# Norm squares added by VectorE, transposes one step later, and a rearranged end in a two-layer hybrid decoder

## The chip, the cores and the metric

The kernel runs on one core of a Trainium2 chip. The core's engines work side by side, each through its own queue in order: TensorE (PE, matmuls, with PEld for its weight loads), VectorE (DVE), ScalarE (ACT), GpSimd (POOL) and SyncE (SP, which here only issues DMAs). The metric is the device time of one execution in microseconds (us); the time of a kernel is the median of several executions. Traces show one profiled execution; its "span" runs from the first to the last instruction.

## The reference, cut to what matters

The input is a sequence of 512 tokens with 1024 channels in float32. Two layers run:

```
layer 0:  h = h + conformer_conv(rmsnorm(h))     # pw1 + GLU, causal depthwise conv of width 31,
                                                 # LayerNorm over channels, swish, pw2
          h = h + swiglu_ffn(rmsnorm(h))         # up 1024 -> 2*2816, silu(gate)*up, down
          k, v = rmsnorm(h) @ w_kv               # one shared K/V
layer 1:  q = rmsnorm(h) @ w_q                   # 16 heads of 64, 4 K/V heads
          s = q k^T / 8 + bias, window of 128 keys, in blocks of 128 queries over 256 keys
          p = exp(s - m) / (sum exp(s - m) + exp(sink - m))
          h = h + (p v) @ w_o
          h = h + swiglu_ffn(rmsnorm(h))
out = rmsnorm(h);   rmsnorm(x) = x * rsqrt(mean(x*x) + 1e-6) * gain
```

## The kernel before, in words

Channels lie on the 128 partitions, tokens along the free dimension: `h` is eight tiles of 128 x 512. Matmuls keep float32 accuracy by splitting both operands into a rounded high part and a low rest: `mm3` (lines 258-264) issues high*high (L262), high*low (L263) and low*high (L264). Weights arrive in chunks of 128 x 1024 (512 KB, DMA at L187); of each chunk ACT makes the high part `whi` (L203) and DVE the low part `wlo` (L204), three chunks ahead of their use. Activations are split by `split_scaled` (ACT L382, DVE L383) or `split` (ACT L386, DVE L387).

In layer 0 the tokens go in two halves of 256. While TensorE works on the first half's `pw2` and FFN, the depthwise convolution of the second half runs in the background: taps on DVE (L611), products on ACT (L603) that POOL adds up (L604), rows of the LayerNorm (L638, L640, L649). The background steps are traced between the weight chunks by due points.

A norm is gathered by the class `Rms`: for each of the eight tiles ACT squares it (L336) and `self.eng`, always POOL, adds it to the running sum (L340). `step1` turns the sum by two small matmuls on PE per half (L350) into a column, DVE scales it (L352), POOL raises it to -1/2 (L354), ACT makes a diagonal (L362); `step2` spreads it over the partitions by a matmul (L375) and ACT copies it out of PSUM (L369). `ffn_up` calls `step1` after the first pair of column blocks (four weight chunks).

Attention (`unit`, line 911) works on units of four heads and 128 queries, eight units for each half `gp` of the heads. A unit is a generator of four stages: scores (PE L927, DVE L930, into a score buffer `sc`, which POOL first gives the sinks, L920); exp with row sums (ACT L937), the reciprocal (DVE L939) and the scaling (POOL L941); transposes (PE L948) with their split (ACT L951, DVE L952); products with V (PE L262 to L264 with `vq`) and their split (ACT L966, DVE L967). `pipeline` (line 970) issues, in step t, the products of unit t-3, the transposes of unit t-2, the exp of unit t-1 and the scores of unit t. Eleven such steps per half; eight of them are traced between the matmuls of the q projection (or of the o projection's first part) and the last three follow behind, by `drain`. `sc` has two buffers. PSUM has eight banks, shared by all.

The end (`Fin`, line 1016) computes the last down projection for the two halves of tokens, `fa` and `fb`. `rows` adds each finished tile to `h` (DVE L1043), squares it (ACT L1047) and sums the squares: in `fa` all eight on POOL (L1049), in `fb` the first four on POOL, and the running sum and the last four go to PE, two small matmuls each (`total`, L1035). `sums` makes the factor (DVE L1066, POOL L1068, DVE diagonal L1070) and lets ACT scale `n_pool` tiles by the gain (L1075): 2 in `fa`, 3 in `fb`. `spread` (L1080) spreads the factor into a PSUM bank; ACT copies it to SBUF (L1082). `out_pool` multiplies the `n_pool` tiles on POOL by the copy (L1089), `out_dve` does the others on DVE straight from the bank (L1095); every tile is stored by a DMA (L1085) from SP, or from ACT for the `out_pool` tiles of `fb`. `fill` places steps of `fa.out_dve` behind given DVE instructions.

The order of the instructions on each engine is chosen by a planner that runs a timeline of its own and takes what is ready, earlier traced work first; semaphores are added by the framework. `issue_after(ins)` keeps what it encloses behind `ins` on the same engine. The framework also orders every two accesses of different engines to one PSUM bank as they were traced, reads among them.

Of the kernel before, what the change touches and what calls it, by code (L numbers as in the profile page):

```python
# [10 lines left out]
F32 = mybir.dt.float32  # L11
# [6 lines left out]
P = 128  # L18
# [3 lines left out]
KT = D // P  # L22
# [6 lines left out]
BAND = 2 * P  # L29
# [120 lines left out]
def hybrid_trunk(ctx: ExitStack, tc: tile.TileContext, xT, W, prm_in, wdw_in, sinks, relb, onehot, outT):  # L150
    nc = tc.nc
# [10 lines left out]
    def uid(s):  # L162
        ctr[0] += 1
        return f"{s}{ctr[0]}"

    def bank():
        return ps.tile([P, 512], F32, tag="bank", name=uid("bank"))
# [4 lines left out]
    def temp():  # L172
        return tmp.tile([P, 512], F32, tag="tmp", name=uid("tmp"))
# [92 lines left out]
    class Act:  # L266
        def __init__(self, n, w=512):
            self.per = 2048 // w
            self.q = [tuple(quads.tile([P, self.per, w], F32R, tag="quad", name=uid("quad")) for _ in range(2))
                      for _ in range(-(-n // self.per))]  # L270
# [6 lines left out]
    ALL = slice(0, S)  # L277
    HALF = (slice(0, 256), slice(256, 512))
# [31 lines left out]
    ones_m = cpool.tile([P, P], F32, tag="ones_m", name="ones_m")  # L310
# [14 lines left out]


    class Rms:
        def __init__(self, bc, tok=ALL):
            self.acc = None
            self.bc, self.tok, self.w = bc, tok, tok.stop - tok.start  # L330
            self.eng = nc.gpsimd
            self.stage = 0

        def add(self, t):
# [43 lines left out]
    def new_bc():  # L378
        return tmp.tile([P, 512], F32, tag="rsbc", name=uid("rsbc"), bufs=2)
# [123 lines left out]
        return hid  # L503

    class Next:
        def __init__(self, gains, x=None, bc=None, tok=ALL):
            self.gains, self.tok = gains, tok
            self.x, self.rms = x, None
            self.bc = bc

        def on_h(self, i):
            if self.x is None:
                self.x = {self.gains[0]: Act(KT)}
            if self.rms is None:
                self.bc = new_bc() if self.bc is None else self.bc
                self.rms = Rms(self.bc, self.tok)
            g = self.gains[0]
            split_scaled(cut(self.x[g][i], self.tok), h[i][:, self.tok], col(g, i))
            self.rms.add(h[i][:, self.tok])
# [28 lines left out]
    with tc.tile_pool(name="conv", bufs=2) as cv:  # L548
# [274 lines left out]
        job(second, (base, 0), (base + 8, 20), (base + 42, h1.n_steps - early))  # L823
        x0 = {"ffn0": Act(KT)}
        bc0 = new_bc()
        n0 = Next(("ffn0",), x0, bc0, HALF[0])
        pw2(h0.z, n0)
        ffn_part(0, 0, x0["ffn0"], HALF[0], n0.rms)
        flush()
# [2 lines left out]
    at = attn.enter_context(tc.tile_pool(name="attn", bufs=2))  # L832
# [25 lines left out]
    if True:  # L858
        ffn_part(0, 1, x0["ffn0"], ALL, Both(), nxt.on_h)
        x, rms = nxt.x, nxt.rms  # L860
# [18 lines left out]
        for half in range(2):  # L879
# [7 lines left out]
            if half == 0:  # L887
                rs_bc = rms.step2()
                rs = rms.rs
                for m in range(2):  # L890
                    t = temp()
# [4 lines left out]
        for n in range(4):  # L896
            t = temp()
# [13 lines left out]
        def unit(gp, jp, n):  # L911
            qt = slice(n * P, (n + 1) * P)
            k0 = max(n - 1, 0) * P
            nk = 1 if n == 0 else 2
            w = nk * P
            rows = [slice(HD * g, HD * (g + 1)) for g in range(2)]
            heads = [gp * 8 + g * 4 + 2 * jp + e for g in range(2) for e in range(2)]
            sc = at.tile([P, 4, 1 + BAND], F32, tag="sc", name=uid("sc"))
            sinks4 = sk.rearrange("p (a g j e) -> p a g j e", a=2, g=2, j=2)[:, gp, :, jp, :]
            nc.gpsimd.tensor_copy(sc[:, :, 0].rearrange("p (g e) -> p g e", g=2), sinks4)  # L920
            m4 = small.tile([P, 4], F32, tag="m4", name=uid("m4"))
            pbs = [bank().rearrange("p (a b) -> p a b", a=2) for _ in range(2)]
            for e in range(2):
                j = 2 * jp + e
                for a, b in ((0, 0), (0, 1), (1, 0)):
                    for g in range(2):
                        nc.tensor.matmul(pbs[g][:, e, :], qs[gp][a][rows[g], j, qt],  # L927
                                         kq[rows[g], b, gp, k0:k0 + BAND], start=a + b == 0, stop=a == 1)
            for u, hd in enumerate(heads):
                nc.vector.tensor_tensor_reduce(  # L930
                    sc[:, u, 1:1 + w], pbs[u // 2][:, u % 2, 0:w], bias[:, hd, BAND - w:BAND],
                    op0=ALU.add, op1=ALU.min, scale=1.0, scalar=sk[:, hd:hd + 1],
                    accum_out=m4[:, u:u + 1])
            yield
            sm = small.tile([P, 4], F32, tag="sm", name=uid("sm"))
            for j in range(4):
                nc.scalar.activation(sc[:, j, 0:1 + w], sc[:, j, 0:1 + w], AF.Exp, bias=m4[:, j:j + 1],  # L937
                                     scale=-1.0, accum_out=sm[:, j:j + 1])
            nc.vector.reciprocal(sm, sm)  # L939
            for j in range(4):  # L940
                nc.gpsimd.tensor_scalar(sc[:, j, 1:1 + w], sc[:, j, 1:1 + w], sm[:, j:j + 1], 0.0,  # L941
                                        op0=ALU.mult, op1=ALU.add)
            yield
            pts = []
            for kb_ in range(nk):
                pt = bank()
                for j in range(4):
                    nc.tensor.transpose(pt[:, j * P:(j + 1) * P], sc[:, j, 1 + kb_ * P:1 + (kb_ + 1) * P], ident)  # L948
                hi = at.tile([P, 512], F32R, tag="pth", name=uid("pth"), bufs=2)
                lo = at.tile([P, 512], F32R, tag="ptl", name=uid("ptl"), bufs=2)  # L950
                nc.scalar.copy(hi, pt)  # L951
                nc.vector.tensor_sub(lo, pt, f32(hi))  # L952
                pts.append((hi, lo))
            yield
            po = bank()[:, 0:BAND]
            for kb_ in range(nk):
                blk = k0 // P + kb_
                for g in range(2):
                    vs = [v[:, blk, gp, 2 * g:2 * g + 2, :].rearrange("p a c -> p (a c)") for v in vq]
                    mm3(po, vs, [pt[:, g * BAND:(g + 1) * BAND] for pt in pts[kb_]],  # L960
                        kb_ == 0 and g == 0, kb_ == nk - 1 and g == 1)
            if os_[gp] is None:
                os_[gp] = (quad(), quad())
            hi, lo = (o[:, 2 * jp:2 * jp + 2, qt] for o in os_[gp])
            src = po.rearrange("p (j q) -> p j q", j=2)
            nc.scalar.copy(hi, src)  # L966
            nc.vector.tensor_sub(lo, src, f32(hi))  # L967
            yield

        def pipeline(gp):  # L970
            units = [unit(gp, jp, n) for n in range(NBLK) for jp in range(2)]
            done = 0
            for t in range(len(units) + 3):
                for d in (3, 2, 1, 0):
                    if 0 <= t - d < len(units):
                        next(units[t - d])
                yield

        def drain(it):
# [36 lines left out]
    class Fin:  # L1016
        def __init__(self, hf):
            self.hf, self.tok = hf, HALF[hf]
            self.banks, self.hg = [bank() for _ in range(4)], []
            self.n_pool = 2 + hf  # L1020

        def down(self, kp, g):
            whi, wlo = get("down", 1, kp, g)
# [13 lines left out]

        def rows(self, g, other=lambda n, ins: None):

            n_add = 4 if self.hf else KT  # L1040
            for i in range(g * 4, g * 4 + 4):
                t = h[i][:, self.tok]
                add = nc.vector.tensor_add(t, self.banks[i // 2][:, (i % 2) * 256:(i % 2) * 256 + 256], t)  # L1043
                if i == KT - 1:
                    other(2, add.ins)
                sq = res.tile([P, 256], F32, tag="sq", name=uid("sq"), bufs=5)
                nc.scalar.square(sq, t)  # L1047
                if 0 < i < n_add:
                    nc.gpsimd.tensor_add(sq, self.acc, sq)  # L1049
                if i < n_add:  # L1050
                    self.run = self.acc = sq
                if not self.hf or i < n_add:
                    continue
                if i == n_add:
                    self.st = bank()
                self.total(sq, i == n_add, i == KT - 1)
                if i == KT - 2:
                    self.total(self.run, False, False)
# [19 lines left out]
        def spread(self):  # L1078
            self.pb = bank()[:, 0:256]
            nc.tensor.matmul(self.pb, ones_m, self.diag, start=True, stop=True)  # L1080
            self.bc = temp()[:, 0:256]
            nc.scalar.copy(self.bc, self.pb)  # L1082

        def store(self, i, t, q=nc.sync):
            q.dma_start(outT[i][:, self.tok], t)  # L1085
# [16 lines left out]
    fa = Fin(0)  # L1102
# [4 lines left out]
    fb = Fin(1)  # L1107
# [7 lines left out]
    for n, (kp, g) in enumerate(steps):  # L1115
        fb.down(kp, g)
        if n == 1:
            fa.sums()
        elif n == 2:
            fb.rows(0)  # L1120
            fa.spread()
        elif n == 3:
            fb.rows(1, fill)
    fa.out_pool()
    fb.sums(fill)
    fb.spread()
# [29 lines left out]
```

## Time and profile before

| | us |
|---|---|
| median of 3 executions | 1123.65 |
| lowest, highest | 1122.11, 1123.83 |
| the profiled execution | 1122.53 |
| its span | 1120.7 |
| PE busy in the span | 1103.7 (98%) |
| DVE, ACT, POOL busy | 663.5, 509.2, 324.0 |

The profiled execution lies 1.1 us under the median. In a group row of the profile, "x4 | 3.6, 952" means four instructions, 3.6 us busy in all, 952 ns each on average; what follows the next bar is the idle time of the engine ahead of them and what ended it. In a row of waits, "A <- B: 3.1, 1, 3.1" means A's engine sat idle until B was done: 3.1 us in all, once, 3.1 us at most. In a timeline row stand start, duration, engine, line, operation, output and inputs; a bracket gives the idle time before it. A row of a table of stretches gives the stretch, its length, then for PE, PEld, DVE, ACT and POOL the busy time and the number of instructions, then the TensorE clock granted, the DMA engines' share and GB/s. A queue's row (SPq, ACTq) counts DMA issues.

### The profile page before, as it was taken

What the parts mean: (1) busy time and instruction counts of PE and PEld (TensorE: products, weight loads), DVE (VectorE), ACT (ScalarE), POOL (GpSimd) and SP (SyncE); (2) the same over time, 40 slices, a digit from 0 to 9 for tenths busy, and PEclk for the clock granted to TensorE, in tenths of its full rate; (3) what the DMA queues carried; (4) which work ended last, traced back from release to release, by engine and by line L of the source; (5) the groups of instructions that cost most, each with busy time, mean ns of one, the idle gap of its engine ahead of it and who ended that gap; (6) DMA issues with size and microseconds to landing.
All of it is one profiled execution on the core that took longest, in us unless ns stands there. A gap on an engine that the chain in (4) does not pass through costs nothing.

```text
span 1120.7 us, 16124 instructions
## 1 busy us (share of the span) xinstructions
PE 1103.7 (98%) x6140; PEld 963.7 (86%) x6140; DVE 663.5 (59%) x1072; ACT 509.2 (45%) x898; POOL 324.0 (29%) x425
## 2 busy tenths in 40 slices
PE   9999998999999999999999999999999999999997
PEld 8888888999999998888888777888888888888886
DVE  4999996977756544533575585674443433444455
ACT  3887787746544322323343564553332211232233
POOL 3999699810200001211230232241111100110014
PEclk9999999999999999999999999999999999999998
DMA  9227054585555542233232111123323232333322
GB/s 357 103 31 83 28 179 133 166 266 177 182 180 181 185 151 95 93 113 94 94 94 93 59 38 39 38 76 98 100 87 110 94 94 94 99 103 100 94 94 76
DMA packets 41722, 128.16 MB, mean 114 GB/s; under 512 B 4491, under 2 KB 12844, under 8 KB 41644
## 3 DMA queue, kind: packets, MB, share of 16 engines
q1 hardware_dynamic: 40924, 126.56, 36.4%
q8 instruction: 48, 0.79, 0.3%
q10 hardware_dynamic: 720, 0.57, 0.2%
q14 instruction: 30, 0.25, 0.1%
HBM read 121.87 MB, written 5.24 MB: 113 GB/s over the span
## 4 chain that ended last, share of the span: by engine, by line
PE 90%; DVE 3%; ACT 3%; issue 2%; POOL 1%; DMA 1%; POOLq 0%; SPq 0%; ACTq 0%; DVEq 0%
PE bank L262 26%; PE bank L263 26%; PE bank L264 25%; PE bank L562 9%; PE bank L927 1%; PE bank L649 1%; PE bank L948 1%; ACT pr L603 1%; POOL pr L604 1%; DVE quad L383 1%; ACT whi L203 1%; DVE wlo L204 0%; DVE bank L611 0%; DVE sc L930 0%; DMA raw<-in_W_dram 0%
## 5 line engine op out<-in xcount | busy, mean ns | idle before, releaser
L263 PE MATMUL bank<-quad,whi 128*128 128x512 f32 (+1 forms) x1584 | 543.6, 343 | 1.7 <-DVE quad L383 1.7
L262 PE MATMUL bank<-quad,whi 128*128 128x512 f32 (+1 forms) x1584 | 543.8, 345 | 0.2
L264 PE MATMUL bank<-quad,wlo 128*128 128x512 f32 (+1 forms) x1584 | 542.9, 343 | 0.0
L204 DVE TENSOR_TENSOR wlo<-raw,whi 128x1024 fp32r<-128x1024 f32 x200 | 269.3, 1347 | 318.2 <-ACT whi L203 310.1
L203 ACT CAST whi<-raw 128x1024 fp32r<-128x1024 f32 x200 | 209.4, 1048 | 355.1 <-PE bank L263 301.2
L263 PEld LDWEIGHTS bank<-quad,whi 128*128 128x128 f32 x1584 | 301.0, 190 | 37.5 <-DVE quad L383 2.8
L262 PEld LDWEIGHTS bank<-quad,whi 128*128 128x128 f32 x1584 | 300.7, 190 | 36.5 <-ACT quad L966 0.6
L264 PEld LDWEIGHTS bank<-quad,wlo 128*128 128x128 f32 x1584 | 300.9, 190 | 34.5 <-DVE wlo L204 0.2
L472 POOL TENSOR_TENSOR tmp<-tmp,tmp 128x512 f32<-128x512 f32 x32 | 45.6, 1425 | 485.1 <-DVE tmp L471 471.5
L604 POOL TENSOR_TENSOR pr<-pr,pr 128x256 f32<-128x256 f32 x208 | 160.5, 822 | 11.0 <-ACT pr L603 11.0
L562 PE MATMUL bank<-quad,w 128*128 128x256 f32 x512 | 114.7, 384 | 0.7 <-DMA w<-in_W_dram 0.7
L611 DVE SCALAR_TENSOR_TENSOR bank<-apad,wdw,bank 128x256 f32<-128x256 f32 x248 | 113.2, 485 | 3.5
L562 PEld LDWEIGHTS bank<-quad,w 128*128 128x128 f32 x512 | 98.5, 193 | 14.9 <-DVE quad L537 0.9
L603 ACT ACTIVATE pr<-apad,wdw 128x256 f32<-128x256 f32 x208 | 99.6, 503 | 23.8 <-POOL pr L604 21.7
L340 POOL TENSOR_TENSOR tmp<-tmp,tmp 128x256 f32<-128x256 f32 (+1 forms) x42 | 45.2, 1076 | 135.2 <-ACT tmp L336 111.1
L470 ACT ACTIVATE tmp<-tmp 128x512 f32<-128x512 f32 x32 | 20.1, 632 | 86.5 <-DVE tmp L469 86.5
L941 POOL TENSOR_SCALAR sc<-sc,sm 128x256 f32<-128x256 f32 (+1 forms) x64 | 30.7, 500 | 86.8 <-DVE sm L939 86.7
L386 ACT CAST quad<-tmp 128x512 fp32r<-128x512 f32 (+1 forms) x48 | 27.8, 584 | 28.9 <-POOL tmp L472 25.0
L471 DVE TENSOR_TENSOR tmp<-bank,rsbc 128x512 f32<-128x512 f32 x32 | 22.1, 691 | 30.1 <-PE bank L264 30.1
L383 DVE SCALAR_TENSOR_TENSOR quad<-h,prm,quad 128x512 fp32r<-128x512 f32 (+1 forms) x40 | 39.4, 1020 | 0.5 <-ACT quad L382 0.4
L937 ACT ACTIVATE sc<-sc,m 128x257 f32<-128x257 f32 (+1 forms) x64 | 30.2, 475 | 15.0 <-DVE m L930 14.8
L387 DVE TENSOR_TENSOR quad<-tmp,quad 128x512 fp32r<-128x512 f32 (+1 forms) x48 | 31.0, 651 | 2.3 <-ACT quad L386 2.3
(137 smaller groups left out, 748.6 us busy)
## 6 DMA issues: line engine op xcount, KB each, us to landing
raw<-in_W_dram SPq DMA_DIRECT2D x208, 512.0 KB, 3.5
w<-in_W_dram SPq DMA_DIRECT2D x15, 512.0 KB, 9.7
fd<-fs SPq DMA_DIRECT2D x1, 3072.0 KB, 33.8
h<-in_xT_dram SPq DMA_DIRECT2D x8, 256.0 KB, 6.3
bias<-fd SPq DMA_DIRECT2D x8, 256.0 KB, 7.2
out_dram<-res SPq DMA_DIRECT2D x13, 128.0 KB, 1.8
w<-in_W_dram SPq DMA_DIRECT2D x2, 256.0 KB, 4.3
out_dram<-res ACTq DMA_DIRECT2D x3, 128.0 KB, 2.4
```

The source lines that it names most:

```text
L203: nc.scalar.copy(hi, r)
L204: lo_engine[0].tensor_sub(lo, r, f32(hi))
L262: nc.tensor.matmul(out, w[0], x[0], start=start, stop=False)
L263: nc.tensor.matmul(out, w[0], x[1], start=False, stop=False)
L264: nc.tensor.matmul(out, w[1], x[0], start=False, stop=stop)
L340: self.eng.tensor_add(sq, self.acc, sq)
L383: nc.vector.scalar_tensor_tensor(dst[1], src, g, f32(dst[0]), op0=ALU.mult, op1=ALU.subtract)
L472: nc.gpsimd.tensor_mul(t2, t1, t2)
L562: mm = nc.tensor.matmul(self.pb[:, w * W2:(w + 1) * W2], w1[ct][:, w, k, :], x[k] if x else xg[k][:, tok], start=k == 0, stop=k == KT - 1)
L603: on_act = nc.scalar.mul(pr, a[:, j:j + W2], tap(j))
L604: on_pool = nc.gpsimd.tensor_add(pr, acc, pr)
L611: on_dve = nc.vector.scalar_tensor_tensor(yt if i == nd - 1 else c, src, tap(i), c if i else self.shift, op0=ALU.mult, op1=ALU.add)
```

## The change

Three places are edited.

- `Rms` gets its adding engine as a parameter, and the norm of the first token half ahead of layer 0's FFN passes `nc.vector`: its seven adds (L340) run on DVE. All other norms stay on POOL.
- In `unit` a second `yield` stands between the scaling and the transposes. `pipeline` runs twelve steps instead of eleven and issues, in step t, the products of unit t-4, the transposes of unit t-3, then the exp of unit t-1 (and at once the empty stage behind it) and the scores of unit t. `sc` has three buffers. Four steps instead of three are left to `drain`.
- At the end, `fb` adds five squares on POOL instead of four, so that PE sums four tiles (the running sum and the last three squares) instead of five. `n_pool` is 2 for both halves. `fb.spread` runs the spreading matmul twice into two banks: DVE reads one, ACT copies the other. `fa`'s copy is no longer made in `spread`; it is traced after `fb.rows(1, fill)` and kept behind the last square of `fb` on ACT.

```
     class Rms:
-        def __init__(self, bc, tok=ALL):
+        def __init__(self, bc, tok=ALL, eng=nc.gpsimd):
...
-            self.eng = nc.gpsimd
+            self.eng = eng
...
     class Next:
-        def __init__(self, gains, x=None, bc=None, tok=ALL):
-            self.gains, self.tok = gains, tok
+        def __init__(self, gains, x=None, bc=None, tok=ALL, eng=nc.gpsimd):
+            self.gains, self.tok, self.eng = gains, tok, eng
...
-                self.rms = Rms(self.bc, self.tok)
+                self.rms = Rms(self.bc, self.tok, self.eng)
...
-        n0 = Next(("ffn0",), x0, bc0, HALF[0])
+        n0 = Next(("ffn0",), x0, bc0, HALF[0], nc.vector)
...
-            sc = at.tile([P, 4, 1 + BAND], F32, tag="sc", name=uid("sc"))
+            sc = at.tile([P, 4, 1 + BAND], F32, tag="sc", name=uid("sc"), bufs=3)
...
                                         op0=ALU.mult, op1=ALU.add)
+            yield
             yield
             pts = []
...
-            for t in range(len(units) + 3):
-                for d in (3, 2, 1, 0):
+            for t in range(len(units) + 4):
+                for d in (4, 3, 1, 0):
                     if 0 <= t - d < len(units):
                         next(units[t - d])
+                        if d == 1:
+                            next(units[t - d])
                 yield
...
-            self.n_pool = 2 + hf
+            self.n_pool = 2
...
-            n_add = 4 if self.hf else KT
+            n_add = 5 if self.hf else KT
...
-                nc.scalar.square(sq, t)
+                self.squared = nc.scalar.square(sq, t).ins
...
         def spread(self):
             self.pb = bank()[:, 0:256]
             nc.tensor.matmul(self.pb, ones_m, self.diag, start=True, stop=True)
+            if self.hf:
+                pb = bank()[:, 0:256]
+                nc.tensor.matmul(pb, ones_m, self.diag, start=True, stop=True)
+                self.copy(pb)
+
+        def copy(self, pb):
             self.bc = temp()[:, 0:256]
-            nc.scalar.copy(self.bc, self.pb)
+            nc.scalar.copy(self.bc, pb)
...
             fb.rows(1, fill)
+    with tc.issue_after(fb.squared):
+        fa.copy(fa.pb)
     fa.out_pool()
     fb.sums(fill)
     fb.spread()
```

## The prediction

> **What bounds the kernel now.** I read the page first, then the waits, then tables of stretches around the longest waits of PE, and the timelines of the engines in them.
>
> ```profile
> span 1120.7 us, 16124 instructions
> ...
> PE 1103.7 (98%) x6140; PEld 963.7 (86%) x6140; DVE 663.5 (59%) x1072; ACT 509.2 (45%) x898; POOL 324.0 (29%) x425
> ...
> PE 90%; DVE 3%; ACT 3%; issue 2%; POOL 1%; DMA 1%; POOLq 0%; SPq 0%; ACTq 0%; DVEq 0%
> ```
>
> PE sets the time: it is busy for 98% of the span and makes 90% of the chain. An edit that removes no matmul can gain only what PE stands still or runs slowly. The change touches three such places. First the norm, by the waits of the stretch from 160 to 210 us, the timelines of PE, ACT and POOL, and a table of stretches:
>
> ```profile
> DVE wlo L204 <- ACT whi L203: 9.4, 7, 2.8
> ACT pr L603 <- POOL pr L604: 7.2, 9, 1.9
> ...
> PE bank L350 <- POOL tmp L340: 3.1, 1, 3.1
> ...
> PE bank L263 <- DVE quad L383: 0.9, 3, 0.4
> ...
> PEld bank L264 <- DVE wlo L204: 0.2, 1, 0.2
> ```
> ```profile
> 169.07 0.40 ACT L336 ACTIVATE tmp<-h 128x256 f32<-128x256 f32 x1
> ```
> ```profile
> 177.81 0.72 POOL L340 TENSOR_TENSOR tmp<-tmp,tmp 128x256 f32<-128x256 f32 x1
> ```
> ```profile
> 178.58 0.61 PE L350 MATMUL bank<-ones_c,tmp 128*128 128x1 f32 x4 [3.10 <-POOL tmp L340]
> ```
> ```profile
> 175.00:180.00 5.00, 1.90 (x16) 1.70 (x15) 2.29 (x2) 3.44 (x7) 5.00 (x7) 0.99 0.42 145
> 180.00:185.00 5.00, 5.00 (x32) 5.00 (x31) 2.97 (x4) 3.19 (x6) 5.00 (x5) 0.67 0.36 117
> 185.00:190.00 5.00, 5.00 (x42) 4.95 (x42) 3.49 (x6) 3.82 (x8) 5.00 (x7) 1.00 0.44 120
> ...
> 200.00:205.00 5.00, 5.00 (x43) 4.91 (x42) 4.96 (x8) 5.00 (x12) 5.00 (x6) 1.00 0.33 105
> ```
>
> The last square is ready at 169.5, its add on POOL ends only at 178.5, since POOL is full (5.00 of 5.00) with the convolution's adds, which stand between. PE waits 3.1 us in L350. Then the granted clock falls to 0.67 over 180 to 185: 32 matmuls run there against 42 in the next five us, ten fewer at 5.00/42 = 0.12 us, or 1.2 us. So the late sum costs 3.1 + 1.2 = 4.3 us.
>
> **The norm's adds on DVE.** Seven adds leave POOL and join DVE. From 165 to 180 us, by groups on POOL and on DVE, and DVE's own price for such an operation (two SBUF inputs of 128x256), from the whole program by shape:
>
> ```profile
> L604 POOL TENSOR_TENSOR pr<-pr,pr 128x256 f32<-128x256 f32 x13 | 13.7, 1078 | 0.0
> L340 POOL TENSOR_TENSOR tmp<-tmp,tmp 128x256 f32<-128x256 f32 x4 | 4.1, 1024 | 0.0
> ```
> ```profile
> L204 DVE TENSOR_TENSOR wlo<-raw,whi 128x1024 fp32r<-128x1024 f32 x5 | 8.3, 1652 | 4.9 <-ACT whi L203 4.9
> L383 DVE SCALAR_TENSOR_TENSOR quad<-h,prm,quad 128x256 fp32r<-128x256 f32 x4 | 3.6, 952 | 0.0
> ```
> ```profile
> L387 DVE TENSOR_TENSOR quad<-tmp,quad 128x256 fp32r<-128x256 f32 x8 | 3.3, 421 | 0.0
> ```
>
> An add on DVE takes 0.42 us where POOL is quiet, and 0.95 at worst, the price of L383, which here runs beside POOL's adds. Four fall behind 165 us: 1.7 to 3.8 us of DVE time, against 4.9 us that DVE idles there waiting for `whi`. By the timeline DVE starts its four L383 here:
>
> ```profile
> 167.55 3.58 DVE L383 SCALAR_TENSOR_TENSOR quad<-h,prm,quad 128x256 fp32r<-128x256 f32 x4
> ```
>
> With the four adds among them, all at the worst price, the sum is ready at 167.55 + 8 x 0.95 = 175.2, still ahead of PE's need at 178.58 - 3.10 = 175.5. So L350's wait goes and with it the slow clock: -4.3.
>
> What is late next is L383. PE already waits 0.9 us for it, and by the traced order the adds of tiles 4, 5 and 6 stand between its four instances. The last low part comes 3 x 0.42 = 1.3 to 3 x 0.95 = 2.9 us later. PE has other products of the same chunks to do, so it may lose nothing, or all 2.9. I take 1.4, near the lower price, because part of it is covered. The part is worth -2.9, between -4.3 and -1.4. The three earlier adds (before 155 us) cost nothing while the operands they delay are early.
>
> Does PE keep this? It would reach the next tight place sooner, by timelines of DVE and PE:
>
> ```profile
> 206.19 1.22 DVE L204 TENSOR_TENSOR wlo<-raw,whi 128x1024 fp32r<-128x1024 f32 x1
> ...
> 207.46 0.38 PE L264 MATMUL bank<-quad,wlo 128*128 128x256 f32 x1
> ```
>
> The weight's low part ends at 207.41 and PE takes it at 207.46: nothing to spare, with DVE at 4.96 and ACT at 5.00 of 5.00 from 200 to 205. The low parts must therefore come earlier by as much as PE does. What holds them is ACT's queue, which waits for POOL's adds (7.2 us in L603), and DVE, which waits for ACT (9.4 us in L204). POOL loses 7 adds, 4.1 us in the last four alone, so both may run ahead by about 4 us, and DVE's 9.4 idle us cover the 3.8 it gets. I take it that the gain is kept.
>
> [...]
>
> **Attention.** By the table of stretches (mains among the steps up to 654, then the first half's last steps alone; the same to 708 and 723.2), and the waits from 645 to 725:
>
> ```profile
> 619.00:654.00 35.00, 35.00 (x211) 27.89 (x210) 22.86 (x73) 21.08 (x62) 9.95 (x24) 1.00 0.18 60
> 654.00:670.00 16.00, 14.03 (x103) 11.48 (x102) 12.41 (x33) 11.26 (x33) 8.09 (x16) 1.00 0.11 34
> ...
> 708.00:723.20 15.20, 14.43 (x105) 12.04 (x102) 12.37 (x39) 11.85 (x37) 5.87 (x14) 1.00 0.11 36
> ```
> ```profile
> POOL sc L920 <- PE bank L948: 16.1, 7, 7.7
> ...
> PE bank L263 <- DVE ptl L952: 1.3, 2, 0.7
> ...
> PE bank L262 <- ACT pth L951: 0.6, 1, 0.6
> ...
> PE bank L948 <- POOL sc L941: 0.6, 1, 0.6
> ```
>
> PE loses time only where no projection is left to mix in. At the 5.00/43 = 0.116 us of the row from 200 to 205, its 103 and 105 matmuls would take 12.0 and 12.2 us: 4.0 and 3.0 lost. DVE needs 12.4 us in each, so at most 3.6 + 2.8 = 6.4 can go. Of the seen waits, the later transposes remove 0.6 (L948 behind L941); the other 1.9 are products behind their splits, which the change leaves back to back with the transposes. What is new is that scores no longer wait for the transposes two units before (16.1 us in L920): these are issued when their input is long ready. Against it, one more unit's transposes and products go into each bare end. If nothing covers their split (0.59 on ACT, 0.69 on DVE by the rows L951 and L952 below), each end loses 1.3: +2.6. Between -6.4 and +2.6 I take -1.3: the two ends give a little, since four units in flight fill more than three, but the split's waits stay.
>
> ```profile
> L952 DVE TENSOR_TENSOR ptl<-bank,pth 128x512 fp32r<-128x512 f32 x28 | 18.9, 686 | 6.3 <-ACT pth L951 6.0
> ...
> L951 ACT CAST pth<-bank 128x512 fp32r<-128x512 f32 x28 | 15.8, 587 | 10.2 <-PE bank L948 8.0 <-PE bank L264 1.9
> ```
>
> **The end.** Timelines of ACT, DVE, POOL and PE:
>
> ```profile
> 1109.54 0.37 ACT L1082 COPY tmp<-bank 128x256 f32<-128x256 f32 x1 [0.60 <-PE bank L1080]
> 1109.81 0.72 ACT L1047 ACTIVATE sq<-h 128x256 f32<-128x256 f32 x2
> ```
> ```profile
> 1114.94 2.05 DVE L1095 SCALAR_TENSOR_TENSOR res<-h,prm,bank 128x256 f32<-128x256 f32 x5 [0.94 <-ACT tmp L1082]
> ```
> ```profile
> 1112.06 0.71 POOL L1068 TENSOR_TENSOR rs<-ms,mhalf 128x2 f32<-128x2 f32 x1 [0.66 <-DVE ms L1066]
> 1114.98 2.09 POOL L1089 TENSOR_TENSOR res<-res,tmp 128x256 f32<-128x256 f32 x3 [2.22 <-ACT tmp L1082]
> ```
> ```profile
> 1109.34 2.44 PE L1035 MATMUL bank<-ones_c,sq 128*128 128x1 f32 x20
> 1113.28 1.22 PE L1080 MATMUL bank<-tmp,ones_m 128*128 128x256 f32 x2 [1.50 <-DVE tmp L1070]
> ```
>
> Gains: four of 20 row-sum passes go (4 x 2.44/20 = 0.5), the last squares no longer stand behind `fa`'s copy (0.3, overlapping), DVE starts 0.4 earlier because it reads another bank than ACT, and POOL has one product fewer (0.7). Costs: the second spread (1.2 on PE at that pace) ahead of POOL's start; a sixth product on DVE (2.05/5 = 0.4) and its store on SP. The added wait: `fa`'s copy on ACT stands behind the last square and behind DVE's first two reads of the bank, hence until about 1110.7 instead of 1109.5; POOL's two `fa` products wait for it, and behind them in POOL's queue may stand L1068, on which the factor hangs: two products at 0.7 from 1111.1 end at 1112.5, 0.45 after L1068's start now. Sum: -0.6 with L1068 ahead, +1.0 behind and nothing hidden; I take +0.2.
>
> The last matmuls' pace is a matter of the clock too. [...]
>
> **Sum.** -2.9 - 1.3 + 0.2 = -4.0. The profiled execution (1122.53, span 1120.7) becomes 1118.5; it lies 1.1 under the median, so for the median 1123.65 - 4.0 = 1119.7.
>
> **Rivals.**
> - *The stall moves.* PE waits for L383 and the other delayed low parts nearly as long (part one -1.4), attention nothing, end +0.2: 1122.5. For it: PE's 0.9 wait there; against: DVE's idle time.
> - *The bare ends give it back.* Part one as forecast, attention +2.6, end +0.2: 1123.55. For it: three of the four seen waits are behind splits; against: L920's 16.1.
> - *DVE becomes the bound: slower.* At the place with nothing to spare (207.4 us) the low parts come later by the four contended adds, 4 x 0.95 = 3.8, and PE with them; attention -1.3, end +0.2: 1126.35. It decides if ACT's `whi` from 194 to 205 do not come earlier, so that DVE cannot use its idle time. For it: DVE and ACT full from 200 to 205; against: POOL's relief.
> - *All goes well.* -4.3, attention -4, end -0.6: 1114.75.
>
> **How the numbers follow.** A measurement can tell 0.2% (2.2 us) from no change, so faster means under 1121.4. Chances: forecast 0.52, all well 0.14, the moved stall 0.11, the bare ends 0.10, DVE the bound 0.13. Faster: 0.52 + 0.14 + 0.02 from rivals in part = 0.68; same 0.19; slower 0.13. The range reaches from the good case to just above the bare ends: 1114.8 to 1124.4; the forecast's own is 1117.0 to 1121.4.
>
> **What would show it.** No wait of PE in L350 near 175 and a clock of 1.00 from 180 to 185; L383's wait in PE's row above 0.9; low parts from 194 to 208 ready earlier by 3 to 4 us; PE's lost time in attention's two bare ends; L1068's place behind or ahead of L1089; L1095 starting with the spread's end. Wrong it would be if the planner orders other work otherwise, or if PE meets the low parts unready near 200.

## The result and the profile after

| | before | after |
|---|---|---|
| median, us | 1123.10 | 1118.96 |
| lowest, highest | 1121.84, 1123.83 | 1118.27, 1121.27 |
| profiled execution | 1122.53 | 1121.16 |

Seven executions of each: the ratio is 0.9972, 95% interval 0.9961 to 0.9983. The change takes 4.1 us off; 4.0 were forecast. The total came out right and two of its three parts did not, as the stretches show.

The page of the kernel after: its span and busy times.

```profile
span 1119.4 us, 16122 instructions
...
PE 1103.5 (99%) x6138; PEld 965.2 (86%) x6138; DVE 670.1 (60%) x1080; ACT 508.6 (45%) x897; POOL 319.0 (28%) x418
```

The profiled execution lies 2.2 us above its own median, so page must not be set against page. Two lines cut the program into stretches. The view of one line's instructions gives their count, their shortest, median and longest duration in ns, and the start of the first and of the last; here L927 (score matmuls) and L350 (row sums of the norms, the convolution's own left out), before and then after:

```profile
L927 PE MATMUL bank<-kq,quad x192: 271/278/384, 619.4 to 715.1; 64*128 64x256 f32 x192
L350 PE MATMUL bank<-ones_c,tmp x28: 164/250/271, 42.6 to 757.9; 128*128 128x1 f32 x28
```
```profile
L927 PE MATMUL bank<-kq,quad x192: 271/278/384, 622.2 to 711.6; 64*128 64x256 f32 x192
L350 PE MATMUL bank<-ones_c,tmp x28: 164/250/250, 44.9 to 756.2; 128*128 128x1 f32 x28
```

Four stretches follow, in us: the start, up to the first L350 (42.6, 44.9); A, from there to the first L927, with the norm in it (576.8, 577.3); B, from there to the last L350, which is attention (138.5, 134.0); C, from there to the end of the span (362.8, 363.2). So in these two executions the start costs 2.3, the norm's stretch 0.5 and the end 0.4, and attention brings 4.5. The start is code that the change leaves alone. PE does less there in the one execution, at a granted clock of 1.00 in both, by the tables of stretches of before and then of after: 27 matmuls from 10 to 15 us against 18.

```profile
10.00:15.00 5.00, 5.00 (x27) 4.46 (x26) 0.16 (x1) 0.00 (x0) 1.38 (x3) 1.00 1.06 390
```
```profile
10.00:15.00 5.00, 5.00 (x18) 4.14 (x17) 0.99 (x2) 0.00 (x0) 2.21 (x4) 1.00 1.06 393
```

**The norm.** Waits from 160 to 215 us, the timeline of DVE, and a table of stretches, all of after:

```profile
PE bank L263 <- DVE quad L383: 2.9, 2, 1.9
...
PE bank L264 <- DVE wlo L204: 0.8, 1, 0.8
```
```profile
171.07 0.94 DVE L383 SCALAR_TENSOR_TENSOR quad<-h,prm,quad 128x256 fp32r<-128x256 f32 x1
171.94 0.95 DVE L340 TENSOR_TENSOR tmp<-tmp,tmp 128x256 f32<-128x256 f32 x1
172.81 1.81 DVE L383 SCALAR_TENSOR_TENSOR quad<-h,prm,quad 128x256 fp32r<-128x256 f32 x2
174.55 0.95 DVE L340 TENSOR_TENSOR tmp<-tmp,tmp 128x256 f32<-128x256 f32 x1
175.42 0.95 DVE L383 SCALAR_TENSOR_TENSOR quad<-h,prm,quad 128x256 fp32r<-128x256 f32 x1
176.29 1.82 DVE L340 TENSOR_TENSOR tmp<-tmp,tmp 128x256 f32<-128x256 f32 x2
```
```profile
170.00:175.00 5.00, 2.12 (x11) 1.73 (x10) 5.00 (x6) 4.56 (x11) 5.00 (x6) 0.85 0.54 188
175.00:180.00 5.00, 4.91 (x23) 4.61 (x22) 4.90 (x6) 3.27 (x6) 5.00 (x6) 0.50 0.00 0
```

L350 no longer waits. In its place PE waits 2.9 us for L383, whose four instances now have adds between them, each at 0.95 with POOL busy throughout (5.00 of 5.00 in both rows). Then the granted clock halves as it did before, only earlier and for longer: 0.50 over the whole of 175 to 180, 23 matmuls in five us. The clock is either 1.00 or 0.50 in the traces of before and after (last section), so that with 0.97 from 180 to 185 the rows add up to 2 x (0.15 + 0.50 + 0.03) x 5 = 6.8 us at half clock, where the two of before (0.99 and 0.67) give 3.4. A wait of 0.8 us for L204 at 207 us comes on top.

**Attention.** Groups on PE from 617 to 726.5 us of before, from 617 to 727 of after:

```profile
L927 PE MATMUL bank<-kq,quad 64*128 64x256 f32 x192 | 22.2, 297 | 0.0
L948 PE MATMUL bank<-ident,sc 128*128 128x128 f32 x112 | 17.3, 278 | 0.6 <-POOL sc L941 0.6
L263 PE MATMUL bank<-ptl,vq 128*128 128x256 f32 x54 | 16.6, 308 | 1.3 <-DVE ptl L952 1.3
L262 PE MATMUL bank<-pth,vq 128*128 128x256 f32 x55 | 16.5, 299 | 0.7 <-ACT pth L951 0.6
```
```profile
L262 PE MATMUL bank<-quad,whi 128*128 128x512 f32 x75 | 29.3, 406 | 0.5 <-ACT quad L967 0.5
...
L927 PE MATMUL bank<-kq,quad 64*128 64x256 f32 x192 | 20.5, 296 | 0.0
L263 PE MATMUL bank<-ptl,vq 128*128 128x256 f32 x56 | 17.8, 317 | 0.8 <-DVE ptl L953 0.8
...
L949 PE MATMUL bank<-ident,sc 128*128 128x128 f32 x112 | 15.4, 273 | 0.0
```

The idle time behind inputs goes from 2.6 to 1.3 us in these rows. More of the gain lies inside busy time: the same 112 transposes keep PE busy for 15.4 us instead of 17.3, the same 192 score matmuls for 20.5 instead of 22.2. These differences can't be added up, since the busy times of two groups overlap: a matmul is shown about 0.28 us long where the next starts 0.12 us later (L262 at 660.42 and L263 at 660.54, before). PE as a whole, over exactly stretch B, idles for 2.8 us before and 1.4 after, and is busy for 135.7 and 132.6 us with the same matmuls (804 and 805 in the records): 1.4 + 3.1 = 4.5.

**The end.** Timelines of DVE, POOL and PE, after:

```profile
1109.92 0.16 DVE L1069 TENSOR_SCALAR ms<-bank 128x2 f32<-128x2 f32 x1 [0.99 <-PE bank L1038]
...
1113.16 2.66 DVE L1105 SCALAR_TENSOR_TENSOR res<-h,prm,bank 128x256 f32<-128x256 f32 x6 [0.43 <-PE bank L1083]
```
```profile
1109.41 1.41 POOL L1099 TENSOR_TENSOR res<-res,tmp 128x256 f32<-128x256 f32 x2 [1.45 <-ACT tmp L1092]
1110.78 0.71 POOL L1071 TENSOR_TENSOR rs<-ms,mhalf 128x2 f32<-128x2 f32 x1
```
```profile
1112.91 1.06 PE L1087 MATMUL bank<-tmp,ones_m 128*128 128x256 f32 x2
```

The power (L1068 before, L1071 after) stands behind `fa`'s two products: its input is ready at 1110.08, it starts at 1110.78. DVE starts its outputs with the first spread's end; the second spread takes 1.06 us. These times go with the clock: `fa`'s spread, two such matmuls as well, takes 0.59 us at 1.00 (at 1108.9 before, 1107.2 after); `fb`'s takes 1.22 at 0.50 before (at 1113.28), and the first of its two 1.12 after, at a mean of 0.57 from 1112 to 1113.

### The profile page after: what moved, and what is told of

The parts are those of the page before. It is cut to its first block, busy times and chain, and to the rows that moved or that the text cites. A ratio compares the mean times of both kernels' runs of the same rounds, so it can differ in the third digit from the quotient of the medians.

```text
span 1119.4 us, 16122 instructions
## 1 busy us (share of the span) xinstructions
PE 1103.5 (99%) x6138; PEld 965.2 (86%) x6138; DVE 670.1 (60%) x1080; ACT 508.6 (45%) x897; POOL 319.0 (28%) x418
## 4 chain that ended last, share of the span: by engine, by line
PE 87%; issue 4%; DVE 3%; ACT 3%; POOL 2%; DMA 0%; SPq 0%; POOLq 0%; ACTq 0%
PE bank L262 25%; PE bank L263 25%; PE bank L264 25%; PE bank L562 9%; POOL pr L604 1%; PE bank L927 1%; PE bank L649 1%; ACT pr L603 1%; PE bank L949 1%; DVE quad L383 1%; DVE bank L611 0%; DMA h<-in_xT_dram 0%; DVE wlo L204 0%; DVE sc L930 0%; PE bank L375 0%
## 5 line engine op out<-in xcount | busy, mean ns | idle before, releaser
L263 PE MATMUL bank<-quad,whi 128*128 128x512 f32 (+1 forms) x1584 | 543.9, 343 | 3.8 <-DVE quad L383 3.7
L262 PE MATMUL bank<-quad,whi 128*128 128x512 f32 (+1 forms) x1584 | 543.6, 345 | 0.5 <-ACT quad L967 0.5
L204 DVE TENSOR_TENSOR wlo<-raw,whi 128x1024 fp32r<-128x1024 f32 x200 | 269.5, 1348 | 315.7 <-ACT whi L203 307.3
L263 PEld LDWEIGHTS bank<-quad,whi 128*128 128x128 f32 x1584 | 301.5, 190 | 39.6 <-DVE quad L383 4.9
L262 PEld LDWEIGHTS bank<-quad,whi 128*128 128x128 f32 x1584 | 301.2, 190 | 36.3 <-ACT quad L967 0.9
L604 POOL TENSOR_TENSOR pr<-pr,pr 128x256 f32<-128x256 f32 x208 | 162.4, 819 | 11.0 <-ACT pr L603 11.0
L340 POOL TENSOR_TENSOR tmp<-tmp,tmp 128x256 f32<-128x256 f32 (+1 forms) x35 | 38.7, 1106 | 138.2 <-ACT tmp L336 114.1
L383 DVE SCALAR_TENSOR_TENSOR quad<-h,prm,quad 128x512 fp32r<-128x512 f32 (+1 forms) x40 | 39.5, 1020 | 0.5 <-ACT quad L382 0.4
```

The source lines that it names most:

```text
L204: lo_engine[0].tensor_sub(lo, r, f32(hi))
L262: nc.tensor.matmul(out, w[0], x[0], start=start, stop=False)
L263: nc.tensor.matmul(out, w[0], x[1], start=False, stop=False)
L340: self.eng.tensor_add(sq, self.acc, sq)
L383: nc.vector.scalar_tensor_tensor(dst[1], src, g, f32(dst[0]), op0=ALU.mult, op1=ALU.subtract)
L604: on_pool = nc.gpsimd.tensor_add(pr, acc, pr)
```

## The experiments

The table sets the stretches of every kernel that ran beside its ratio to the kernel before, which ran again beside each (medians 1122.9 to 1123.4). Each stretch is worked out from the kernel's own rows of L350 and of the score matmuls (L927, on another line in some) and its span as above.

| kernel | median | ratio (95%) | A | B | C |
|---|---|---|---|---|---|
| before | | | 576.8 | 138.5 | 362.8 |
| after | 1118.96 | 0.9972 (0.9961 to 0.9983) | 577.3 | 134.0 | 363.2 |
| norm's edit alone | 1123.22 | 1.0001 (0.9992 to 1.001) | 577.4 | 138.5 | 362.9 |
| attention's edit alone | 1118.04 | 0.9951 (0.9938 to 0.9963) | 577.9 | 133.9 | 362.3 |
| end's edit alone | 1122.95 | 1.0001 (0.9993 to 1.001) | 577.6 | 138.5 | 363.2 |
| after without norm's edit | 1119.27 | 0.9962 (0.995 to 0.9975) | 576.8 | 133.9 | 363.2 |
| third score buffer alone | 1122.60 | 0.9998 (0.9989 to 1.0007) | 576.8 | 138.4 | 362.3 |
| adds behind L383 | 1122.62 | 1.0 (0.9991 to 1.0009) | 577.4 | 138.6 | 362.3 |
| L350 later | 1124.54 | 1.0009 (1.0 to 1.0018) | 578.9 | 138.5 | 362.4 |
| attention, L350 later | 1119.91 | 0.9977 (0.9968 to 0.9986) | 579.1 | 134.0 | 362.8 |
| adds behind L383, L375 later | 1126.58 | 1.003 (1.0018 to 1.0043) | 580.3 | 138.5 | 362.9 |
| the same with attention | 1122.18 | 0.9993 (0.9984 to 1.0002) | 583.0 | 134.0 | 362.3 |
| attention, L354 first, 8 steps | 1117.80 | 0.9955 (0.9942 to 0.9969) | 576.8 | 134.0 | 362.9 |
| attention, L354 first, 4 steps | 1119.77 | 0.9971 (0.996 to 0.9983) | 579.8 | 134.0 | 362.3 |

Where a kernel leaves a stretch's code alone, B repeats within 0.2 us, C within 0.6, A within 1.1. A's spread goes with the time at half clock (last section): A is 576.8 in the three kernels with PE at half clock for 3.4 us behind L350's stall (before, the third buffer, after without the norm's edit), and 577.6 and 577.9 in the two with 6.8 us (the end's edit, attention's edit).

**Each edit alone.** The edits are the three places of the change:

```
norm:       n0 = Next(("ffn0",), x0, bc0, HALF[0], nc.vector)
attention:  sc ... bufs=3; yield, yield; range(len(units) + 4); for d in (4, 3, 1, 0)
end:        n_add = 5; n_pool = 2; two spreads; fa.copy(fa.pb) behind fb.squared
```

> The kernel before with the norm's edit alone. The prediction's sum: -2.9 us, no wait of PE in L350 and a clock of 1.00 from 180 to 185. The rival that the traces of the two whole kernels suggest: the stall only moves to L383 (1.9 + 1.0 us of waits of PE near 172), the granted clock is halved for about as long as before or longer, and a wait for L204 near 207 comes on top: between -0.5 and +1.0 us against the kernel before.

> The kernel before with attention's edit alone. The prediction's sum: -1.3 us. The rival by the distances between equal matmuls in the two traces: -4.6 us, 2.7 of it in the first half of the heads and 1.9 in the second, since scores and transposes then fill nearly all that PE lost in the bare ends.

> The kernel before with the end's edit alone. The prediction's sum: +0.2 us (between -0.6 and +1.0). By the traces of the two whole kernels: +0.35, L1068 standing behind the two products of the first half on POOL. Both say no change that can be told from none; over +1.0 or under -0.6 refutes both.

> The changed kernel without the norm's edit (attention and end alone). The prediction's sum: -1.1 us against the kernel before, so 2.9 slower than the changed kernel. The rival, by which the norm's edit is worth nothing: -4 us, as fast as the changed kernel or up to 1 us faster.

The norm's edit is worth nothing that can be measured, alone (1.0001) or within the change (0.9962 without it, 0.9972 with it; A 576.8 and 577.3). Its waits from 160 to 215 us, and the table of stretches:

```profile
PE bank L263 <- DVE quad L383: 2.7, 2, 1.9
...
PE bank L264 <- DVE wlo L204: 1.2, 1, 1.2
```
```profile
170.00:175.00 5.00, 3.90 (x16) 3.31 (x17) 5.00 (x7) 3.95 (x9) 5.00 (x6) 0.56 0.37 105
```

2.7 + 1.2 us of waits take the place of 3.1 + 0.9, and PE is at half clock for 6.8 us (0.56 in the row above, 0.76 in the next) in place of 3.4. At equal slow time, against the 577.6 and 577.9 above, A's 577.4 would be a gain of 0.2 to 0.5 us, too little for the medians to tell. Attention's edit brings about 4.5 us of stretch B in every kernel that has it (133.9 to 134.0 against 138.4 to 138.6) and, alone, the whole of the gain. The end's edit costs 0.3 to 0.9 in C (363.2 in all three kernels that have it, 362.3 to 362.9 in the others), too little for the medians to tell.

**Which half of attention's edit.** The third buffer without the later transposes; the later transposes can't stand without the third buffer, since three units' scores are then alive.

```
-            sc = at.tile([P, 4, 1 + BAND], F32, tag="sc", name=uid("sc"))
+            sc = at.tile([P, 4, 1 + BAND], F32, tag="sc", name=uid("sc"), bufs=3)
```

> The kernel before with a third score buffer alone; transposes stay where they are. If L920's wait for the transposes of two units before (16 us of POOL's time) was what cost PE time: -2 us or more. If the gain of attention comes from the later transposes (no product and no transpose close behind its input) and L920's wait is idle time of an engine that bounds nothing: within 0.5 us of before.

B is 138.4: nothing. And in the kernel after, whose B is 134.0, the row of waits that the prediction built on is still there (645 to 725 us; 16.1 before):

```profile
POOL sc L920 <- PE bank L949: 15.6, 7, 4.3
```

With the third buffer alone it stays at 16.1 us, so that run does not try what the wait costs. But B is 4.5 us shorter with 15.6 us of it left: the gain does not come from its going. It belongs to the later transposes, with the buffer that they need. That it comes from PE finding its inputs ready fits the waits and busy times above, but no run tries it apart.

**Why the norm's edit gains nothing.** First suspicion: the adds stand between the L383. Here the last four adds are traced behind the last L383.

```
+            with tc.issue_after(ins):                      # ins: L383 of the last tile
+                for sq in self.sqs if i == KT - 1 else []:
+                    self.eng.tensor_add(sq, self.rms.acc, sq)
+                    self.rms.acc = sq
```

> The norm's edit alone, but the last four adds are kept behind the last of the four L383 on DVE. If the gain went because the adds stood between the L383: the waits of PE for L383 shrink to the 0.9 us of before, L350 keeps no wait over 1 us, the granted clock stays at 1.00 and the kernel is 2 to 3 us faster than before (the prediction's -2.9 plus the 1.4 it gave to L383, less up to 1.2 near 207 us). If it went because four contended adds on DVE are too much at this place, wherever they stand: within 1 us of before, with waits of PE for L204 in place of those for L383.

And the same stall removed with no load on DVE: adds on POOL, but L350 traced one weight chunk later.

```
+                    if half == 0 and which == 0 and w == 256 and pair == lo + 1:
+                        rms.step1()
...
-                rms.step1()
+                if tok.start:
+                    rms.step1()
```

> The kernel before, adds on POOL, but the two row sums of this norm (L350) are traced one weight chunk later, so that PE needs the sum 24 matmuls x 0.12 = 2.8 us later. If the stall of PE in L350 and the slow clock behind it were worth 4.3 us, this shows it without any load on DVE: L350 waits 0.3 us, the clock stays at 1.00, -3 to -4.3 us. If the place near 207 us has nothing to spare (as the rival of the prediction had it), PE comes there 4 us earlier with ACT and POOL no earlier, and waits there instead: -1 to 0 us.

> Attention's edit together with the later L350, adds on POOL and the end as before. If the two gains add: 1118.0 for attention alone, less 3 to 4.3, so about 1114 to 1115. If the later L350 gains nothing: 1118.0 within 0.8.

Neither gains. With the adds behind L383 the clock is 1.00 in every row of five us from 165 to 220, but PE waits 5.6 us instead of 4.0. The later L350 loses 2.1 us of A against the kernel before, with attention's edit 2.3; PE is at half clock for 6.8 us in both (0.82 and 0.50 in the rows from 185 to 195, with attention's edit 0.73 and 0.59). Waits of PE from 160 to 215 us, first with the adds behind L383, then (to 225) with the later L350:

```profile
PE bank L375 <- ACT tmp L362: 2.5, 1, 2.5
PE bank L263 <- DVE quad L383: 1.8, 3, 1.3
PE bank L264 <- DVE wlo L204: 1.3, 1, 1.3
```
```profile
PE bank L375 <- ACT tmp L362: 4.6, 1, 4.6
...
PE bank L350 <- POOL tmp L340: 0.3, 1, 0.3
```

Both remove L350's wait, but for 0.3 us, and meet a wait that the kernel before does not have: L375, the spread, for the diagonal that hangs on L354 by way of ACT. POOL's timeline before, and with the adds behind L383, shows why:

```profile
178.49 5.16 POOL L604 TENSOR_TENSOR pr<-pr,pr 128x256 f32<-128x256 f32 x6
183.62 1.69 POOL L354 TENSOR_TENSOR rs<-ms,mhalf 128x2 f32<-128x2 f32 x1
```
```profile
173.57 9.61 POOL L613 TENSOR_TENSOR pr<-pr,pr 128x256 f32<-128x256 f32 x9
...
184.82 0.70 POOL L354 TENSOR_TENSOR rs<-ms,mhalf 128x2 f32<-128x2 f32 x1
```

(L613 is L604 there.) The place that the adds left on POOL is filled by the convolution. L354 ends at 185.5 instead of 185.3, although PE no longer waits 3.1 us for the sum. Before, PE came to L375 only at 186.6, behind its stall in L350, and found the diagonal ready; now it comes 2.5 us too early and starts L375 at 186.3.

**Moving the next wait too.** On top of the adds behind L383, the first evacuation, which calls the spread, comes two chunks later, alone and with attention's edit.

```
-                    if half == 0 and which == 1:
+                    if w == 256 and tok.start == 0:
+                        drop = half == 1 and which == 1
+                    else:
+                        drop = half == 0 and which == 1
+                    if drop:
```

> As the last four adds kept behind L383 on DVE, and the evacuation of the first pair of column blocks, which calls the spread (L375), is traced two weight chunks later: L375 then stands 35 matmuls x 0.12 = 4.2 us further back on PE. If the chain L352, L354 (POOL), L362 is what ate the gain of the norm's edit (2.5 us of wait of PE in L375 with the adds behind L383), that wait is gone and the kernel is about 2.5 us faster than before, unless the low parts near 203 us (1.3 us of wait for L204) take it back. If the sum of all work of POOL, ACT and DVE bounds this stretch, some other wait grows by as much: within 0.8 us of before.

> The same with attention's edit, the end as before. If the gains add: 1118.0 for attention alone less 2.5, so 1115.5; if the norm's stretch gives nothing: 1118.0 within 0.8.

The wait in L375 goes and A grows by 3.5. Waits of PE from 160 to 235 us:

```profile
PE bank L262 <- ACT whi L203: 2.6, 2, 1.3
PE bank L263 <- DVE quad L383: 1.9, 1, 1.9
...
PE bank L262 <- ACT rsbc L369: 1.4, 1, 1.4
PE bank L264 <- DVE wlo L204: 1.2, 1, 1.2
```

Smaller waits stand in its place, 2.6 + 1.9 + 1.4 + 1.2 = 7.1 us against 5.6 with the adds behind L383 and 4.0 before: the weights' parts and the spread's copy are now late. With attention's edit A is worse still (583.0).

**Taking the convolution out of the way.** With attention's edit, adds on POOL as before; the convolution's steps traced from here on are kept behind L354, and fewer of them (8 or 4 instead of 20) are due by the eighth chunk.

```
-        job(second, (base, 0), (base + 8, 20), (base + 42, h1.n_steps - early))
+        job(second, (base, 0), (base + 8, 8), (base + 42, h1.n_steps - early))
...
+                    self_h1[0].after = self_h1[0].after + [rms.pow]
```

> Attention's edit, the end as before, all adds of the norm on POOL; but the convolution's steps traced from here on are kept behind this norm's L354 on POOL, and 8 instead of 20 of them are due by the eighth chunk, so that the last four adds and L354 follow each other on POOL. If what holds PE here is the order on POOL alone (the sum, then L354, each behind the convolution's adds): no wait over 1 us in L350 or L375, clock 1.00, 1118.0 less 3 to 4, so 1114 to 1115. If ACT, whose products wait for POOL, and DVE behind it bound the stretch: other waits (for L203 or L204) as large, 1118.0 to 1121.

> The same with 4 steps due by the eighth chunk: still less of the convolution stands ahead of the adds on ACT, DVE and POOL. By the order of POOL: as the run with 8, or up to 1 us faster; by the bound of the helpers: within 1 us of it, since the same work only moves behind.

At its own place this works in part: with 8 steps L354 starts at 176.63, and PE waits neither in L350 nor in L375. It waits 1.5 us for L383, where the waits of before add up to 4.0, and is at half clock for 3.4 us, as before. But the convolution's work is still to be done. Tables of stretches behind that place, before and then with 8 steps:

```profile
215.00:240.00 25.00, 25.00 (x205) 24.79 (x203) 21.17 (x29) 12.50 (x17) 7.69 (x8) 1.00 0.70 214
240.00:265.00 25.00, 25.00 (x205) 24.52 (x205) 20.62 (x39) 16.79 (x29) 0.71 (x1) 1.00 0.75 250
```
```profile
215.00:240.00 25.00, 24.23 (x194) 23.61 (x193) 23.71 (x36) 15.35 (x24) 14.73 (x15) 1.00 0.55 166
240.00:265.00 25.00, 23.25 (x181) 22.01 (x180) 18.75 (x31) 11.66 (x17) 3.54 (x6) 1.00 0.81 257
```

POOL's work there rises from 8.4 to 18.3 us, and PE, which waits for nothing from 215 to 300 in the kernel before, now does. Its waits with 8 steps, from 160 to 300:

```profile
PE bank L653 <- POOL y L619: 1.7, 2, 1.4
PE bank L263 <- DVE quad L383: 1.5, 2, 1.3
...
PE bank L264 <- DVE wlo L204: 0.6, 1, 0.6
```

L653, the LayerNorm's sums (L649 before), waits 1.7 us for the convolution's result, and a low part is late by 0.6. What was won ahead of 215, 4.0 - 1.5 = 2.5 us, is given back by 2.3, the slow time is the same, and A is 576.8 to the tenth. (The 35 matmuls that the rows have fewer are no measure of the loss, since matmuls differ in length: in the kernel before L649 takes 0.38 us, a product 0.28.) With 4 steps it is worse: one wait, for the LayerNorm of the convolution, is alone 4.0 us (waits from 215 to 300), and A is 579.8.

```profile
PE bank L684 <- ACT tmp L680: 4.0, 1, 4.0
```

So five ways of removing L350's stall (on DVE among the splits, on DVE behind them, L350 later, L375 later too, L354 first) leave A at 576.8 to 583.0. The gain that the first theory of each expectation foresaw came in none. The second theory of each, that other waits grow in place of the one removed, fits better. That what sets PE's loss from 165 to 290 us is then the work of the convolution on ACT, DVE and POOL, and not the order at one place, is argued and not shown: no kernel with less of that work was run. The second theories also said too little of the harm: the later L350 cost 1 us by its ratio where -1 to 0 was expected, and with attention's edit 1.9 by the medians (1119.91 against 1118.04) where 0.8 was the bound; the later L375 cost 3.2, and with attention's edit 4.1, where 0.8 was the bound; 4 steps cost 2.0 more than 8 where 1 was. Part of the later L350's harm may be the clock, at 0.50 for 6.8 us against 3.4 before; with attention's edit it is 6.8 against 6.9.

Attention's edit alone (0.9951) and with 8 steps (0.9955) have lower medians than the kernel after (0.9972); the intervals overlap, so that they beat it is not shown.

## Why the prediction was right, and where it was not

The total was right by luck, because two errors of opposite sign cancel: the norm, -2.9 forecast, about nothing measured; attention, -1.3 forecast, -4.5 measured; the end, +0.2 forecast, +0.3 to +0.9 measured in C.

- **The norm, the part that failed.** Four sentences did. "I take 1.4, near the lower price, because part of it is covered": L383's wait grew by 2.9 - 0.9 = 2.0 us, since the adds stand among the four L383 and DVE began them later (171.07, against 167.55 before; the late start of this execution explains 2.3 of the 3.5). The other 1.2 speak against "The three earlier adds (before 155 us) cost nothing": they take 0.94 to 0.95 each, and DVE, which idled for 0.60 + 0.54 us between them and L383 in the kernel before, does not idle there any more. With the adds behind L383 and the same three adds, L383 began 0.6 later, counted from the first L350 (167.68 - 42.1 against 167.55 - 42.6); why not 1.2 is open. And "So L350's wait goes and with it the slow clock": the wait went and the slow clock did not; it followed PE's new waits and lasted 6.8 us instead of 3.4. Its price was too low as well: the 1.2 are the row from 180 to 185 alone, and 3.4 us at half clock are 1.7 us of matmuls, an estimate from the kernel after, where PE ran 23 in the five us at 0.50 and 44 from 195 to 200 at 1.00. What I took for certain, -4.3, was the wrong part. "I take it that the gain is kept" fails even where L383 is left in peace: I looked for the next tight place at 207 us and passed over the chain from the same sum to L375, twenty us nearer, whose L354 stands in the same full POOL queue. For this part the rival "the stall moves" was the right one, and dearer than its -1.4: it gave everything back.
- **207 us.** The row with nothing to spare was read rightly: PE waits 0.8 at this time in the kernel after, one chunk earlier in the program, and 1.2 for L204 with the norm's edit alone. It is a part of the loss, not the 3.8 of the rival by which DVE becomes the bound; low parts that come 3 to 4 us earlier, which the forecast needed there, did not come: the L204 that PE waits for in the kernel after ends at 207.16 (before: 204.29), counted from the first L350 0.6 later than before, and takes 1.78 us instead of 1.26.
- **The price of an add on DVE.** Six of the seven took 0.94 to 0.95 us, the upper end of the range and not a mixture, the last 0.77; POOL ran L604 without a gap beside the last four (159.45 to 186.81). With all adds at 0.95 the forecast's own terms give -4.3 + 2.9 = -1.4 for this part: that came nearer, and still promised a gain that did not come.
- **Attention: right in direction, wrong in mechanism and size.** L920's wait stayed (15.6 us) and the third buffer alone gave nothing. I let the seen waits (2.6 us in the groups) and an upper bound by DVE's busy time stand for what PE lost, and took the gain low because "the split's waits stay"; they halved. The rival by which the bare ends give it back saw new waits behind those splits; PE's idle time in B fell from 2.8 to 1.4. The larger part, 3.1 us, was in PE's busy time for the same matmuls, the transposes and scores among them, which was part of the 4.0 + 3.0 us that I had counted as lost in the bare ends. I had no row that told how much of this the new order would free, and chose near the low end. That is the term that was mis-sized: -1.3 for -4.5. PE's busy share of 98% did not show it: in B its busy time is 135.7 us before and 132.6 after, for the same matmuls.
- **The end.** L1071 behind the products of `fa` was the dearer of the two orders that I weighed, and it came so: 0.7 us of delay. C came out 0.3 to 0.9 us longer, within the -0.6 to +1.0 of the two orders; the other terms can't be told apart in it.

## What to carry to other kernels

A stall that a helper engine causes is a place where lateness is visible, not the amount that can be won: ask what the same helpers owe PE next, follow that chain through every queue it crosses, and count all their work up to where they have slack. Compare two traces by the distances between the same instructions, stretch by stretch; a right total can be two wrong terms. The busy time of a fixed number of matmuls, set against the same number elsewhere, shows lost time that no row of waits shows (here 3.1 us in B); take PE as a whole for it, since the busy times of groups overlap. And count the time at half clock before two stretches are compared: between kernels with the same code there, A was 0.8 to 1.1 us longer where that time was 6.8 us than where it was 3.4.

## What the runs showed of the hardware

In the traces of before and after the granted clock is 1.00 or 0.50 in every stretch of half a us but those in which it changes. It falls twice in each. In before it is at 0.50 for 3.4 us from 179.9 and again from 1111.7 to the end of the span, in after for 6.8 us from 173.5 and again from 1112.1 to the end. Around the first fall, before and then after:

```profile
175.00:179.90 4.90, 1.80 (x16) 1.60 (x15) 2.19 (x2) 3.38 (x6) 4.90 (x7) 1.00 0.41 140
179.90:183.30 3.40, 3.40 (x18) 3.40 (x18) 1.37 (x3) 2.20 (x4) 3.40 (x5) 0.50 0.35 102
183.40:188.00 4.60, 4.60 (x40) 4.54 (x39) 3.22 (x4) 3.62 (x9) 4.60 (x6) 1.00 0.46 160
```
```profile
170.00:173.40 3.40, 0.93 (x6) 0.54 (x4) 3.40 (x4) 3.07 (x9) 3.40 (x4) 1.00 0.61 201
173.50:180.30 6.80, 6.40 (x28) 6.11 (x29) 6.70 (x8) 4.67 (x9) 6.80 (x7) 0.50 0.07 30
180.40:185.00 4.60, 4.60 (x41) 4.60 (x40) 2.92 (x4) 4.11 (x6) 4.60 (x4) 1.00 0.79 229
```

So a row of five us with a mean clock c holds 2 x (1 - c) x 5 us of half clock, if the clock has these two values alone. For before the prediction's rows, 0.99 and 0.67, give 2 x (0.01 + 0.33) x 5 = 3.4, as its trace has it. For the other kernels the rows of five us are what was read, and the time at half clock is an estimate from them. The same stall of 3.1 us in L350, in code that was not touched, was followed by 3.4 us in three kernels (before, the third buffer, after without the norm's edit) and by 6.8 to 6.9 us in two (the end's edit, attention's edit). For attention's edit:

```profile
175.00:180.00 5.00, 2.02 (x9) 2.02 (x10) 2.88 (x2) 3.29 (x6) 5.00 (x6) 0.80 0.36 113
180.00:185.00 5.00, 5.00 (x26) 5.00 (x25) 2.94 (x5) 3.03 (x6) 5.00 (x6) 0.51 0.30 105
```

These give 2 x (0.20 + 0.49) x 5 = 6.9. A is 0.8 to 1.1 us longer in the two kernels with the longer slow time. Why the same stall is followed by 3.4 us in one run and by twice as much in another, no run shows.

The length of the wait did not tell either whether the clock falls. In the kernel with L375 later, no single wait of PE from 160 to 235 us is longer than 1.9 us, yet the clock in this row is 0.66, with 23 matmuls in five us:

```profile
170.00:175.00 5.00, 4.61 (x23) 4.15 (x24) 4.93 (x7) 3.94 (x9) 5.00 (x6) 0.66 0.35 105
```

With attention and 8 steps the clock was 0.89 and 0.77 in the rows from 165 to 175 (3.4 us), and the waits of PE from 160 to 215 us are two, of 1.5 us in all. With the adds behind L383, a wait of 2.5 us in L375 left it at 1.00 in every row from 165 to 220. So from these runs the cost of one stall is known beforehand only to about 1 us, the 0.8 to 1.1 by which A differs.
